# A 90-degree rotation of an 8192x8192 matrix: macro tiles of 512 whole rows in place of 1024 half rows

## The chip, the core and the metric

The kernel runs on one core of a Trainium2 chip. The metric is the device time of one execution in microseconds (us), lower being better. The work of the core is spread over engines that run beside each other, each with its own queue of instructions in a fixed order: TensorE (PE; loading its weights is listed apart as PEld), VectorE (DVE), ScalarE (ACT), GpSimd (POOL) and SyncE (SP). Transfers between the main memory and the on-chip memory (SBUF) are issued by SP and ACT and carried out by 16 DMA engines, which both share. Everything waits for each other through semaphores.

## The reference

The input is a matrix of 8192x8192 float32 numbers (268.44 MB), and the output is the matrix turned by 90 degrees against the clock.

```python
def setup_inputs():
    return {"x": np.random.randn(8192, 8192).astype(np.float32), "k": 1}

def reference(x, k):
    return np.rot90(x, k)
```

So `out[M-1-c, r] = x[r, c]`: a column of the input becomes a row of the output, and the last column becomes the first row. Nothing is computed on the numbers; each is read once and written once, 536.87 MB in all.

## The kernel before

**Macro tiles.** The matrix is cut into macro tiles of `R` = 1024 rows by `W` = 4096 columns, 16 MB each, in `macro_tiles`. There are 16 of them; the last is cut into two of 512 rows (`LAST = [4, 4]`, in units of 128 rows). A macro tile is loaded whole before most of its output can be stored, because a stored run holds one value from each of its rows.

**Load.** `load` brings in 128 rows at a time. Each load (L102, issued by SP) moves 128 rows of 16 KB, 2 MB, into a landing tile `a`, one row to a partition. VectorE then copies the tile in 8 chunks of 512 columns into tiles `ar` (L108), reversing the order of the columns inside each block of 128. In what follows this copy is called a flip.

**Store.** `store` goes over the 32 blocks of 128 columns of a macro tile, `G` = 4 blocks to an output tile. For each block TensorE transposes the eight 128x128 squares (L148) into a PSUM tile `pt`; a PSUM tile holds `PW` = 2 blocks, 2048 numbers to a partition, half of PSUM. ScalarE copies it into the output tile `ot` (L169), and after the second copy it issues the store of 2 MB (L177). Each partition holds 16 KB of the output tile, which goes to four output rows: four runs of 1024 numbers, 4 KB. `whole_reads` (L23) rewrites the reading side of each store from four pieces to one contiguous piece of 16 KB to a partition; the writing side keeps its four runs. With `rows` = 512, in the two last macro tiles, an output tile has 8 blocks, and each partition writes eight runs of 2 KB.

**Buffers.** `a_pool` has 2 landing tiles of 16 KB to a partition, `r_pool` 63 flipped chunks of 2 KB, `o_pool` 3 output tiles of 16 KB, `psum_pool` 2 tiles of 8 KB. A macro tile has 64 chunks, one more than `r_pool` holds. A buffer is taken again as soon as its last reader is done, in the order in which buffers come free. So a load waits until the flips of the load two before it are done; a flip waits for its load and for the transposes that read the buffer it takes; a transpose waits for its flips and for a free PSUM tile; the copies of an output tile wait for the transposes and for the landing of the store that used the buffer before, which is the store three before.

**The two ends.** In the first macro tile some loads land in tiles of `o_pool` (L97), the transposes of the first output tile run row block by row block as these land (L158), and two of the first stores are split in halves (L139). In the two last macro tiles every other output tile is taken from `a_pool` (L131), the flips of the last rows are put ahead of the second output tile (L190 to L200), and the last store is split in halves.

Of the kernel before, what the change touches and what calls it, by code (L numbers as in the profile page):

```python
# [2 lines left out]

# [5 lines left out]

P = 128  # L10

R = 1024
RT = R // P
LAST = [4, 4]
W = 4096
CH = 512
F = 4096  # L20
FP = 2048


def whole_reads(nc):

    for fn in nc.m.functions:
        for block in fn.blocks:
            for n, ins in enumerate(block.instructions):
                if not isinstance(ins, mybir.InstDMACopy):
                    continue
                src = ins.ins[0]
                ap = [list(d) for d in src.ap]
                if len(ap) == 3 and ap[2][0] == 1 and ap[1][0] == ap[2][1]:
                    ap = [ap[0], [1, 1], [1, ap[1][1] * ap[2][1]]]
                    block.instructions[n] = copy.replace(  # L40
                        ins,
                        ins=[copy.replace(src, ap=ap)],
                        ant_dge_precooked=False,
                    )


def macro_tiles(N, M):

    tiles = [(r0, RT, c0) for r0 in range(0, N, R) for c0 in range(0, M, W)]
    r0, _, c0 = tiles.pop()  # L50
    for n in LAST:
        tiles.append((r0, n, c0))
        r0 += n * P
    return tiles


@with_exitstack
def kernel(
    ctx: ExitStack,
    tc: tile.TileContext,  # L60
    x: bass.AP,
    k: bass.AP,
    out: bass.AP,
):
    nc = tc.nc
    assert k == 1, f"only k=1 supported, got {k}"
    nc.at_finalize(whole_reads)

    N, M = x.shape
    dt = x.dtype  # L70

    consts = ctx.enter_context(tc.tile_pool(name="consts", bufs=1))
    ident = consts.tile([P, P], dt)
    make_identity(nc, ident)

    a_pool = ctx.enter_context(tc.tile_pool(name="a_pool", bufs=2))
    r_pool = ctx.enter_context(tc.tile_pool(name="r_pool", bufs=63))
    o_pool = ctx.enter_context(tc.tile_pool(name="o_pool", bufs=3))
    psum_pool = ctx.enter_context(
        tc.tile_pool(name="psum", bufs=2, space=bass.MemoryType.PSUM)  # L80
    )

    loads = 0

    def load(r0, rt, c0):

        nonlocal loads
        chunks = {}
        for t in range(rt):


            if loads < RT and loads % 5 >= 2:  # L97
                a = o_pool.tile([P, W], dt, tag="o")
            else:
                a = a_pool.tile([P, W], dt, tag="a")  # L100
            loads += 1
            nc.sync.dma_start(  # L102
                out=a[:], in_=x[r0 + t * P : r0 + (t + 1) * P, c0 : c0 + W]
            )
            yield chunks
            for j in range(W // CH):
                ar = r_pool.tile([P, CH // P, P], dt, tag="ar")
                nc.vector.tensor_copy(  # L108
                    out=ar[:],
                    in_=a[:, j * CH : (j + 1) * CH].rearrange(  # L110
                        "r (b m) -> r b m", m=P
                    )[:, :, ::-1],
                )
                chunks[t, j] = ar
            yield chunks

    def store(r0, rt, c0, chunks, end):

        rows = rt * P
        PW = 1
        while 2 * PW * rows <= FP:
            PW *= 2
        G = PW
        while 2 * G * rows <= F:
            G *= 2
        for i, g0 in enumerate(range(0, W // P, G)):  # L130
            if end and i % 2 == 0:  # L131
                ot = a_pool.tile([P, F], dt, tag="a")
            else:
                ot = o_pool.tile([P, F], dt, tag="o")
            o = ot[:, : G * rows].rearrange("m (g f) -> m g f", g=G)

            lead = r0 == 0 and c0 == 0 and i in (4, 6)  # L139
            S = PW if lead or (end and r0 + rows == N and g0 + G == W // P) else G  # L140


            ps = {}

            def transposes(t, ws):
                for w in ws:
                    g = g0 + w
                    nc.tensor.transpose(  # L148
                        ps[w // PW][:, PW - 1 - w % PW, t * P : (t + 1) * P],
                        chunks[t, g * P // CH][:, g % (CH // P), :],  # L150
                        ident,
                    )

            def psum_tile(h):
                pt = psum_pool.tile([P, FP], mybir.dt.float32, tag="ps")
                ps[h] = pt[:, : PW * rows].rearrange("m (g f) -> m g f", g=PW)

            if i == 0 and (rt == RT or r0 + rows < N):  # L158
                for h in range(G // PW):
                    psum_tile(h)  # L160
                for t in range(rt):
                    transposes(t, range(G))
            for h in range(0, G, PW):
                if h // PW not in ps:
                    psum_tile(h // PW)
                    for w in range(h, h + PW):
                        for t in range(rt):
                            transposes(t, [w])
                nc.scalar.copy(o[:, G - PW - h : G - h, :], ps[h // PW])  # L169

                done = h + PW
                if done % S == 0:
                    top = M - c0 - (g0 + done) * P
                    dst = out[top : top + S * P, r0 : r0 + rows].rearrange(
                        "(g m) f -> m g f", g=S
                    )
                    nc.scalar.dma_start(  # L177
                        out=dst, in_=o[:, G - done : G - done + S, :]
                    )
            yield  # L180

    tiles = macro_tiles(N, M)
    *most, before_last, last = tiles
    for m in most:
        *_, chunks = load(*m)
        for _ in store(*m, chunks, False):
            pass


    *_, chunks = load(*before_last)  # L190
    outputs = store(*before_last, chunks, True)
    rows = load(*last)
    for _ in range(2 * last[1] - 1):
        next(rows)
    next(outputs)
    chunks = next(rows)
    for _ in outputs:
        pass
    for _ in store(*last, chunks, True):
        pass  # L200


# [1 line left out]
_INS = ['x', 'k']  # L204
_OUTS = [((8192, 8192), 'float32')]

_NUMBERS = {'k': 1}


# [26 lines left out]
```

## Time and profile before

The time is the median of 2 runs. The profile is of one execution of the same program; its span runs from its first to its last instruction.

| | |
|---|---|
| time, median (lowest to highest) | 1267.76 us (1267.45 to 1268.06) |
| span of the profiled execution | 1266.1 us |
| read and written | 268.44 MB and 268.44 MB, 424 GB/s over the span |
| PE, 4096 transposes | busy 718.2 us, 57% of the span |
| PE weight loads, 4096 | busy 678.6 us, 54% |
| ACT, 256 copies of 128x2048, 1869 ns each | busy 466.7 us, 37% |
| DVE, 1024 flips of 128x512 | busy 355.4 us, 28% |
| DVE waits for loads | 524.0 us in 82 waits |
| loads: 128 of 2 MB | 16.8 us from issue to landing (median) |
| stores: 125 of 2 MB, 6 of 1 MB | 25.5 and 27.3 us from issue to landing (median) |

How to read it: busy time is the time in which an engine works on an instruction, and an engine that is idle is waiting for a semaphore. A DMA is issued in well under a microsecond by SP or ACT; its landing is the moment at which the last of the 16 DMA engines has reported. The profile also records each packet, the piece that one DMA engine moves at a time: here one row of 16 KB of a load, or the 16 KB of one partition of a store (8 KB for a half store), and one small packet of 4 bytes for each DMA and DMA engine that reports the landing. A DMA of 128 rows is 8 packets for each of the 16 engines.

### The profile page before, as it was taken

The page shows a single profiled execution, that of the slowest core. Times are in us where ns is not written, and L with a number is a line of the kernel's source. Part 1 is how long each engine was busy: PE and PEld are TensorE (multiplying, and loading weights), DVE is VectorE, ACT ScalarE, POOL GpSimd, SP SyncE. Part 2 cuts the span into 40 slices and gives each one's busy share as a digit, 9 for nine tenths or more (in the row PEclk, how much of TensorE's full clock was granted, in tenths as well). Part 3 has the DMA queues.
Part 4 walks back from the last instruction along what each step waited for, and adds up shares of the span by engine and source line. Part 5 has one row for each costly group of instructions (what it writes and reads, how often), then busy time and mean ns, then how long its engine had stood idle before and what let it go on. Part 6 is the DMA issues. An engine that isn't in the chain of part 4 may idle for free.

```text
span 1266.1 us, 10392 instructions
## 1 busy us (share of the span) xinstructions
PE 718.2 (57%) x4096; PEld 678.6 (54%) x4096; DVE 355.4 (28%) x1024; ACT 466.7 (37%) x257; POOL 0.7 (0%) x6
## 2 busy tenths in 40 slices
PE   1554565556656665556555665555655656556673
PEld 1543455555555555456554655555655655556562
DVE  4423223222232223222232223322232222322210
ACT  0432433433333333343334333343333433343363
POOL 0000000000000000000000000000000000000000
PEclk9977877777776777867778678677686686776797
DMA  9999999999999999999999999999999999999997
GB/s 399 426 428 430 428 429 427 430 429 429 429 429 429 430 428 427 430 429 430 428 430 428 429 429 428 430 428 428 430 430 428 429 429 428 428 428 428 427 399 328
DMA packets 37345, 537.55 MB, mean 425 GB/s; under 512 B 4144, under 2 KB 4144, under 8 KB 4144
## 3 DMA queue, kind: packets, MB, share of 16 engines
q10 hardware_dynamic: 18864, 268.44, 50.0%
q1 hardware_dynamic: 18432, 268.44, 49.7%
q8 instruction: 32, 0.52, 0.2%
q14 instruction: 17, 0.14, 0.0%
HBM read 268.44 MB, written 268.44 MB: 424 GB/s over the span
## 4 chain that ended last, share of the span: by engine, by line
DMA 82%; ACT 14%; PE 1%; issue 1%; ACTq 1%; DVE 0%; SPq 0%
DMA out_dram<-ot 79%; ACT ot L169 14%; DMA a<-in_x_dram 3%; PE pt L148 1%; ACTq L177 0%; DVE ar L108 0%; ACTq L169 0%; SPq L102 0%
## 5 line engine op out<-in xcount | busy, mean ns | idle before, releaser
L148 PE MATMUL pt<-ident,ar 128*128 128x128 f32 x4096 | 718.2, 356 | 528.0 <-ACT ot L169 487.6
L148 PEld LDWEIGHTS pt<-ident,ar 128*128 128x128 f32 x4096 | 678.6, 191 | 567.4 <-ACT ot L169 521.4
L169 ACT COPY ot<-pt 128x2048 f32<-128x2048 f32 x256 | 465.4, 1869 | 756.7 <-DMA out_dram<-ot 727.0
L108 DVE COPY ar<-a 128x512 f32<-128x512 f32 x1024 | 355.4, 421 | 861.1 <-DMA a<-in_x_dram 524.0
L169 ACT ACT_TABLE_LOAD x1 | 1.3, 1283 | 25.5 <-DVE ar L108 25.5
masks.py:199 POOL TENSOR_SCALAR_AFFINE_SELECT ident<-ident 128x128 f32<-128x128 f32 x1 | 0.3, 292 | 0.1
masks.py:197 POOL MEMSET ident<- 128x128 f32 x1 | 0.2, 204 | 0.3 <-POOLq L217 0.3
L217 POOL MEMSET const-bfloat16-1.0<- 128x1 bf16 x1 | 0.1, 102 | 0.0
L217 POOL MEMSET const-uint8-127<- 128x1 uint8 x1 | 0.1, 102 | 0.0
L217 POOL MEMSET const-float32-0.0<- 128x1 f32 x1 | 0.1, 99 | 0.2 <-issue 0.2
L217 POOL MEMSET const-float32-1.0<- 128x1 f32 x1 | 0.1, 99 | 0.0
## 6 DMA issues: line engine op xcount, KB each, us to landing
a<-in_x_dram SPq DMA_DIRECT2D x128, 2048.0 KB, 16.8
out_dram<-ot ACTq DMA_DIRECT2D x125, 2048.0 KB, 25.5
out_dram<-ot ACTq DMA_DIRECT2D x6, 1024.0 KB, 27.3
```

The costliest lines, as they stand in the source:

```text
L108: nc.vector.tensor_copy(out=ar[:], in_=a[:, j * CH : (j + 1) * CH].rearrange("r (b m) -> r b m", m=P)[:, :, ::-1],)
L148: nc.tensor.transpose(ps[w // PW][:, PW - 1 - w % PW, t * P : (t + 1) * P], chunks[t, g * P // CH][:, g % (CH // P), :], ident,)
L169: nc.scalar.copy(o[:, G - PW - h : G - h, :], ps[h // PW])
L217: nc = _bacc.Bacc("TRN2", target_bir_lowering=False, num_devices=1)
```

## The change

Macro tiles become 512 whole rows: `R` = 512 and `W` = 8192, still 16 MB. `macro_tiles`, `LAST` and the special treatment of both ends go, and the two generators become one plain loop.

- A load moves 128 rows of 32 KB, 4 MB; there are 64 instead of 128. The landing tiles are 32 KB to a partition, still two. A load gives 16 chunks.
- An output tile has `G` = 8 blocks, a PSUM tile `PW` = 4; in bytes both are as before. Each of the 128 stores is 2 MB: 16 KB read from each partition, written as eight runs of 2 KB.
- `r_pool` has 55 chunks instead of 63, `o_pool` two tiles instead of three.
- The counts of flips (1024), transposes (4096) and copies (256) and their shapes stay. In the built program each engine has the same instructions in number; SP has 64 loads, ACT 128 stores, none of them half a store.
- The transposes of an output tile always run block by block, over the four row blocks of a block.

```diff
-R = 1024
+R = 512
 RT = R // P
-LAST = [4, 4]
-W = 4096
+W = 8192
...
-    r_pool = ctx.enter_context(tc.tile_pool(name="r_pool", bufs=63))
-    o_pool = ctx.enter_context(tc.tile_pool(name="o_pool", bufs=3))
+    r_pool = ctx.enter_context(tc.tile_pool(name="r_pool", bufs=55))
+    o_pool = ctx.enter_context(tc.tile_pool(name="o_pool", bufs=2))
...
+    PW = FP // R
+    G = F // R
+    for r0 in range(0, N, R):
         chunks = {}
+        for t in range(RT):
+            a = a_pool.tile([P, W], dt, tag="a")
+            nc.sync.dma_start(out=a[:], in_=x[r0 + t * P : r0 + (t + 1) * P, :])
             for j in range(W // CH):
                 ar = r_pool.tile([P, CH // P, P], dt, tag="ar")
                 nc.vector.tensor_copy(
...
                 chunks[t, j] = ar
+        for g0 in range(0, W // P, G):
+            o = o_pool.tile([P, G, R], dt, tag="o")
             for h in range(0, G, PW):
+                pt = psum_pool.tile([P, PW, R], mybir.dt.float32, tag="ps")
+                for w in range(PW):
+                    g = g0 + h + w
+                    for t in range(RT):
+                        nc.tensor.transpose(
+                            pt[:, PW - 1 - w, t * P : (t + 1) * P],
+                            chunks[t, g * P // CH][:, g % (CH // P), :],
+                            ident,
+                        )
+                nc.scalar.copy(o[:, G - PW - h : G - h, :], pt[:])
+            top = M - (g0 + G) * P
+            nc.scalar.dma_start(
+                out=out[top : top + G * P, r0 : r0 + R].rearrange(
+                    "(g m) f -> m g f", g=G
+                ),
+                in_=o[:],
+            )
```

More of the change, by code (lines that the diff above doesn't have):

```diff
@@ L44, in whole_reads @@
                     )
[L47 to L54, printed above, removed]
 @with_exitstack
@@ L81 @@
     )
-    loads = 0
-    def load(r0, rt, c0):
-        nonlocal loads
+    PW = FP // R
+    G = F // R
+    for r0 in range(0, N, R):
         chunks = {}
[L94 to L105, printed above, removed]
+        for t in range(RT):
+            a = a_pool.tile([P, W], dt, tag="a")
+            nc.sync.dma_start(out=a[:], in_=x[r0 + t * P : r0 + (t + 1) * P, :])
             for j in range(W // CH):
@@ L114, in load @@
                 chunks[t, j] = ar
[L115 to L162, printed above, removed]
-            for h in range(0, G, PW):
[L164 to L200, printed above, removed]
+        for g0 in range(0, W // P, G):
+            o = o_pool.tile([P, G, R], dt, tag="o")
+            for h in range(0, G, PW):
+                pt = psum_pool.tile([P, PW, R], mybir.dt.float32, tag="ps")
[15 more added lines that the diff above has]
+            )
```

## The prediction

> **What bounds the kernel now.** I read the page first: its slices and its table of DMA queues.
>
> ```profile
> DMA  9999999999999999999999999999999999999997
> q10 hardware_dynamic: 18864, 268.44, 50.0%
> q1 hardware_dynamic: 18432, 268.44, 49.7%
> ```
>
> The 16 DMA engines are busy from the first slice to the last. The stores (q10, issued by ACT) and the loads (q1, issued by SP) take 99.7% of the span between them, packet after packet. No compute engine comes near: the fullest, PE, is at 57%. So the time is the sum of the packets' times on a DMA engine, and it falls only if packets get shorter and rises if they get longer or if the DMA engines are left without work.
>
> The table of waits says the same from the other side.
>
> ```profile
> ACT ot L169 <- DMA out_dram<-ot: 727.0, 118, 11.0
> PE pt L148 <- ACT ot L169: 487.6, 128, 9.2
> ```
>
> ACT waits for a store to land and frees its output tile, PE waits for ACT. Each of these waits is harmless as long as other packets are queued meanwhile. That is what three output tiles buy, and the change takes one away. So the third view is the timeline of one output tile in the steady part.
>
> ```profile
> 1137.41 3.64 ACT L169 COPY ot<-pt 128x2048 f32<-128x2048 f32 x2 [6.20 <-DMA out_dram<-ot]
> 1139.33 5.14 PEld L148 LDWEIGHTS pt<-ident,ar 128*128 128x128 f32 x32 [3.45 <-ACT ot L169]
> 1141.08 0.55 ACTq L177 DMA_DIRECT2D out_dram<-ot  x1
> 1144.83 2.77 DVE L108 COPY ar<-a 128x512 f32<-128x512 f32 x8 [7.07 <-PE pt L148]
> 1147.24 3.63 ACT L169 COPY ot<-pt 128x2048 f32<-128x2048 f32 x2 [6.19 <-DMA out_dram<-ot]
> ```
>
> An output tile takes 9.83 us (1137.41 to 1147.24), the time of one load and one store on a DMA engine. From the start of the copies to the issue of the store are 3.67 us. Last, the DMA view of four windows: the steady part, the end, where only stores with 2 KB runs are left, and a stretch with half stores beside loads.
>
> ```profile
> DMA packets 2938, 42.89 MB, mean 429 GB/s; under 512 B 320, under 2 KB 320, under 8 KB 320
> q10 hardware_dynamic: 1469, 21.45, 50.5%
> q1 hardware_dynamic: 1465, 21.38, 50.0%
> ```
>
> ```profile
> DMA packets 519, 7.54 MB, mean 419 GB/s; under 512 B 59, under 2 KB 59, under 8 KB 59
> q10 hardware_dynamic: 518, 7.52, 100.4%
> ```
>
> ```profile
> q1 hardware_dynamic: 238, 3.39, 61.2%
> q10 hardware_dynamic: 285, 2.18, 39.7%
> ```
>
> The first, 400 to 500 us: 21.45 MB of stores are 1309 packets of 16 KB, and 50.5% of 16 engines in 100 us is 808 us, so a store packet with 4 KB runs takes 617 ns. The loads give 613 ns. The second, 1226 to 1244 us: 459 packets in 100.4% of 288 us, 629 ns for a store packet with 2 KB runs (most are 626, where most with 4 KB runs are 615). The third, 88 to 101 us: 8 KB store packets beside 16 KB load packets, and the loads got 61% of the time. The engines alternate packet by packet, not byte by byte: the longer packet gets the larger share.
>
> **Loads: 32 KB packets.** The most frequent packet records are 309 ns for 8 KB and 611 ns for 16 KB, so 302 ns for each further 8 KB and 7 ns for the packet itself. A 32 KB packet is then 1215 ns instead of 1222 for two. Each DMA engine has 512 of them: 512 x 7 ns = -3.6 us, and 64 landing packets fewer at 9 ns, -0.6 us. In sum -4.2. No packet of 32 KB is in the trace; the ends are 0 (two times 611) and, by the slower 616 ns that load packets average from 1100 to 1200 us, +5.
>
> **Stores: 2 KB runs everywhere.** Of the 1024 store packets of a DMA engine, the 64 of the last two macro tiles have 2 KB runs already. 960 x (629 - 617) ns = +11.5 us. The row for 2 KB is from a stretch without loads, so the cost beside loads is not shown: ends 0 and, by the worst of the final full stores (634 ns on average), +16. I take 11.5, the row of the same shape. The Trainium skill, "DMA: Bandwidth & Descriptors", section Specifications, asks only 512 B for line rate, so by it 2 KB runs would cost nothing and the traffic would come out at -4.2; the measured 629 against 617 disagrees, and the measurement decides.
>
> So traffic alone moves 1266.1 to 1266.1 - 4.2 + 11.5 = 1273.4 us.
>
> **Two output tiles: does the queue run dry?** This is the part that could cost most. In the built program a load can be issued once the flips of the load two before are done, and the last of these needs the 13th transpose of a PSUM tile that starts when ACT has made the first copy of an output tile, that is, when a store has landed. So the landing of every second store starts both the next load and the refill of that output tile. I count from this landing on one DMA engine. The refill: 0.08 us to the copies, 3.64 us of copies, 0.02 to the issue, then the delay to the first packet. Of that I have two rows: the first 2 KB store, issued at 1217.25 with no load queued, reported from the first DMA engine 6.58 us later, and 8 x 0.626 = 5.01 of these are its packets: 1.57 us. The run's first store, issued at 47.90 into a stream of loads, sent its first packet at 51.14: 3.24 us. So the refill takes 5.3 to 7.0 us; I take 5.3, since the queue of the stores is in use when it is issued. In this time the other output tile is in the queue: 8 packets alone, 8 x 0.629 = 5.0 us. That is 0.3 us too few, unless packets of a load lie among them. The load: its issue comes at 0.08 + 1.92 (start of copy to start of PE) + some 2 (13 transposes; 16 took 1.97 us at 54.60) + 0.4 (a flip) = 4.4 us, its first packet 3.0 (steady loads) to 3.8 us (the load issued at 52.24, beside a store) later, near 7.9 us. It then alternates with the refilled store at 1.22 + 0.63 us a pair. If that store started at 5.3, it has four packets done before the load joins, and lands with about three load packets, 3.6 us, left to cover the next refill. But that later start lets the load catch up, and the round after has no cover but its own 5.0 us. So rounds with 0.3 us and rounds with none alternate; and 16 engines must now report before one of two tiles is free, where the landings of one store are spread over 16 us (the store at 1141.08 was reported from 9.4 to 25.7 us after issue) and the 32 packets that fetch instructions hold one engine up by about 1 us each. I take 0.2 us a round, ends 0 and 1.9 (7.0 - 5.0 in every round). The Trainium skill, same page and section, gives a first byte after about 0.6 us for DMAs of these two queues; the trace has 1.0 at its fastest (the first load, 0.74 to 1.74), and by the rule the refill would be 4.3 us, under 5.0, with no gap at all.
>
> A round is one load and two stores. Loads 0 to 4 go before the first store (5 x 9.7 us, to about 50 us, as 5 to 10 loads did before), so 59 rounds: 59 x 0.2 = +11.8 us.
>
> **The ends.** Before, the first store is issued at 47.90. Now load 3 lands near 1.7 + 4 x 9.7 = 40.6, then flip, two PSUM tiles and two copies give about 46.7, and load 4 keeps the DMA engines busy till 50: nothing lost, so the removed special cases at the start cost nothing; without that load they would cost the 6 us between. At the end some ten stores are left without loads, before with tiles of `a_pool` to help, now with two: 0.3 us for each pair, +1.5. ACT stays off the path, two copies and an issue being 4.2 us against 5.0 of packets.
>
> **Landing tiles, chunks, engines.** The flips of a load are paced by four PSUM tiles, 19.7 us, and a load of 4 MB lands some 22 us after the store that released it; its first chunk is needed after the next two stores have landed. So DVE and PE are not late, and 55 chunks cost nothing; if a load came over 5 us later than this, PE would wait for it and the gap would become a load's.
>
> Sum: 1273.4 + 11.8 + 1.5 = 1286.7 us of span. The median of the runs is 1.7 us above the span, so 1288.
>
> **Rivals.** *The output tiles run dry in every round.* With a delay of 3.24 us, or a load that starts early enough to share its packets away, each round has a gap of 0.7 to 1.9 us: 1274.9 + 1.7 + 59 x 0.7 to 1.9 = 1318 to 1389. For it: the wait for a landing is ACT's largest. Against it: loads need 3 us and more to start, which leaves cover. It decides from (1293.1 - 1276.6) / 59 = 0.28 us a round, where 2% is passed. *The rows pay.* 2 KB runs cost nothing beside loads and no gap opens: 1266.1 - 4.2 + 1.7 = 1264. For it: in the steady part stores share every moment with loads. Against: the 4 KB runs cost their 4 ns more than loads there too. *The 32 KB rows are cut in two by the hardware.* Then loads and stores alternate in equal packets, a store beside a load lasts 10 us, more than any refill: no gap, 1266.1 + 11.5 + 1.7 = 1279.
>
> A gain of 2% is hardly to be had: at 302 ns for 8 KB with nothing for packets, 536.87 MB over 16 engines take 1237 us, 1242 with the ends.
>
> **Chances.** The forecast with a gap of 0 to 0.5 us a round, 1274 to 1306, has 0.55; dry in every round 0.27; the rows pay 0.08; cut in two 0.09; something unseen and faster 0.01. Of the forecast's 0.55 about 0.15 lies above 2%, which is about what a measurement of this kernel can tell from no change. So slower 0.42, same 0.57, faster 0.01. The range, 1268 to 1325, leaves out most of the rows that pay and the worse half of the dry rounds.
>
> **What would show it.** Load packets of 32 KB near 1215 ns and store packets near 629; alternation of pairs in which loads take two thirds; a round of 19.8 us, with a store landing after about 15 us beside a load and 5 alone; a DMA row with tenths of 9 and a few of 8. Slices of 8 throughout would speak for dry rounds; store packets of 617 would show the second term wrong; 64 loads with 16384 packets of 16 KB, the third rival; waits of PE for DVE, the part on chunks.

## The result and the profile after

The changed kernel takes 1379.9 us (median of 2 runs, 1378.4 to 1381.4) against 1267.8 before: 1.0885 times as long, 95% interval 1.0854 to 1.0917. The forecast was 1288, in a range from 1268 to 1325. The profiled execution has a span of 1376.6 us, 110.5 more than before.

The page of the changed kernel, slices and table of DMA queues (packets, MB, share of 16 engines' span):

```profile
DMA  9999999999999999999999999999999999999988
GB/s 410 408 382 393 374 396 407 388 382 381 401 400 386 388 370 401 405 394 383 390 392 409 381 386 385 393 408 384 380 387 396 407 382 386 383 396 418 392 373 344
q10 hardware_dynamic: 18432, 268.44, 48.5%
q1 hardware_dynamic: 9216, 268.44, 47.2%
```

The row of tenths still shows 9 nearly everywhere, and that is a trap: a 9 begins at 90%. The queues tell more. Before, they filled 99.9% of the span, now 95.8% with the instruction fetches (0.1%). Added up from the packet records, the average DMA engine has 56 us without a packet, where it was 2, and 1320 us of packets, where it was 1264: the packets themselves take longer. So about half of the loss, 54 us, is idle time, and the other half, 56 us, is packet time. The load packets average 1268 ns, though the middle one takes 1214; the store packets average 651 ns, though the middle one takes 624.

From the table of waits (us in total, times, longest):

```profile
ACT o L101 <- DMA out_dram<-o: 784.5, 95, 15.1
DVE ar L82 <- PE pt L96: 694.8, 211, 16.2
PE pt L96 <- ACT o L101: 676.5, 122, 15.0
```

ACT's wait for landings grew from 727.0 us in 118 waits to 784.5 us in 95: fewer waits, longer ones, up to 15.1 us where 11.0 was the longest. The landings no longer come evenly. The timeline shows in what order they come (start, duration, engine; in brackets the idle time before and what ended it):

```profile
590.09 0.33 SPq L79 DMA_DIRECT2D a<-in_x_dram  x1
...
601.59 0.55 ACTq L103 DMA_DIRECT2D out_dram<-o  x1
...
603.37 41.49 SPq L79 DMA_DIRECT2D a<-in_x_dram  x3
...
614.30 3.63 ACT L101 COPY o<-pt 128x2048 f32<-128x2048 f32 x2 [12.75 <-DMA out_dram<-o]
...
627.31 3.64 ACT L101 COPY o<-pt 128x2048 f32<-128x2048 f32 x2 [9.38 <-DMA out_dram<-o]
...
630.98 0.55 ACTq L103 DMA_DIRECT2D out_dram<-o  x1
...
632.94 1.87 ACT L101 COPY o<-pt 128x2048 f32<-128x2048 f32 x1 [2.00 <-PE pt L96]
...
637.12 0.55 ACTq L103 DMA_DIRECT2D out_dram<-o  x1
...
640.48 3.64 ACT L101 COPY o<-pt 128x2048 f32<-128x2048 f32 x2 [3.39 <-DMA out_dram<-o]
```

Before, copies started every 9.83 us. Here they start at 614.3, 627.3, 632.9 and 640.5, and the pattern repeats every 42.9 us on average with two loads and four stores, where packets of the middle lengths would need 39.4 (16 x 1.214 + 32 x 0.624). The two loads come close together: one was issued at 590.09, the next at 603.37 (its row merges three issues, of which the others are at 632.76 and 644.53), and both had landed by 626.6. The next one sends its first packet near 638. Two windows of the DMA view, 604 to 609 and 625 to 637 us, show both halves of the pattern:

```profile
q1 hardware_dynamic: 48, 1.57, 72.8%
q10 hardware_dynamic: 35, 0.57, 26.7%
```

```profile
q10 hardware_dynamic: 302, 4.42, 95.6%
q1 hardware_dynamic: 6, 0.00, 0.0%
```

While loads are queued they take two thirds of the engines and more: 73% in this short window, 66.4% from 600 to 624 us, where 207 load packets and 208 store packets were sent, one for one. Stores crawl meanwhile: the store issued at 601.59 took 25.6 us to land. Then for 12 us no load moves at all (the six packets of the second window only report a landing). In the packet records there are 29 such stretches of more than 2.5 us, 382 us in all; before there were two, of 3.5 and 4.0 us, both in the first 140 us. In the 29 two output tiles must keep 16 DMA engines busy alone. Near 631 us they don't: by 631.2 all engines but one had sent their packets of one store, and the next, issued at 630.98, sent its first packet at 632.2.

### The profile page after: what moved, and what is told of

It reads as the page before. It is cut to its first block, busy times and chain, and to the rows that moved or that the text cites. A ratio compares the mean times of both kernels' runs of the same rounds, so it can differ in the third digit from the quotient of the medians.

```text
span 1376.6 us, 10332 instructions
## 1 busy us (share of the span) xinstructions
PE 648.7 (47%) x4096; PEld 615.2 (45%) x4096; DVE 366.1 (27%) x1024; ACT 468.8 (34%) x257; POOL 0.7 (0%) x6
## 3 DMA queue, kind: packets, MB, share of 16 engines
q1 hardware_dynamic: 9216, 268.44, 47.2%
## 4 chain that ended last, share of the span: by engine, by line
DMA 81%; ACT 10%; issue 8%; PE 1%; DVE 0%; ACTq 0%; SPq 0%
DMA out_dram<-o 78%; ACT o L101 10%; DMA a<-in_x_dram 3%; PE pt L96 1%; DVE ar L82 0%; ACTq L101 0%; SPq L79 0%
## 5 line engine op out<-in xcount | busy, mean ns | idle before, releaser
L96 PE MATMUL pt<-ident,ar 128*128 128x128 f32 x4096 | 648.7, 334 | 717.2 <-ACT o L101 676.5
L96 PEld LDWEIGHTS pt<-ident,ar 128*128 128x128 f32 x4096 | 615.2, 177 | 750.5 <-ACT o L101 707.7
L101 ACT COPY o<-pt 128x2048 f32<-128x2048 f32 x256 | 467.5, 1870 | 898.9 <-DMA out_dram<-o 784.5
L82 DVE COPY ar<-a 128x512 f32<-128x512 f32 x1024 | 366.1, 422 | 962.0 <-PE pt L96 694.8
L101 ACT ACT_TABLE_LOAD x1 | 1.3, 1283 | 0.7 <-PEq L125 0.7
```

The costliest lines, as they stand in the source:

```text
L82: nc.vector.tensor_copy(out=ar[:], in_=a[:, j * CH : (j + 1) * CH].rearrange("r (b m) -> r b m", m=P)[:, :, ::-1],)
L96: nc.tensor.transpose(pt[:, PW - 1 - w, t * P : (t + 1) * P], chunks[t, g * P // CH][:, g % (CH // P), :], ident,)
L101: nc.scalar.copy(o[:, G - PW - h : G - h, :], pt[:])
```

## The experiments

Three theories stood at first: that two output tiles are too few (1), that the 32 KB landing tiles and packets make loads come in bursts (2), that 2 KB runs slow the packets beside loads (3). Ratios are to the kernel before in the same comparison, with 95% intervals.

**e1: the kernel before with two output tiles.**

```diff
-    o_pool = ctx.enter_context(tc.tile_pool(name="o_pool", bufs=3))
+    o_pool = ctx.enter_context(tc.tile_pool(name="o_pool", bufs=2))
```

> The kernel before with two output tiles in place of three, nothing else changed. Theory 1 (two output tiles are too few: from the landing of a store to the first packet of the next store from that tile are some 5 us, as from 627.2 to 632.2 us of the changed kernel, and the one other store does not always cover that): the loss of the change comes back here, 1 to 1.75 us for every two stores, 64 times, so 1330 to 1380 us. Theory 2 (the 32 KB landing tiles and packets are to blame: loads come in bursts and leave stretches with stores alone, in which two output tiles are too few; with 2 MB loads always among the stores two would do): 1268 to 1285 us. Theory 3 (2 KB runs): 1268 us, since the runs here are 4 KB.

Measured: 1272.8 us, ratio 1.0047 (1.0032 to 1.0062). The page's queues:

```profile
q10 hardware_dynamic: 18864, 268.44, 49.9%
q1 hardware_dynamic: 18432, 268.44, 49.7%
```

As full as before: two output tiles alone cost 5 us, and theory 1 falls as the sole cause.

**e2: the changed kernel with loads of half rows into four landing tiles of 16 KB.**

```diff
-            a = a_pool.tile([P, W], dt, tag="a")
-            nc.sync.dma_start(out=a[:], in_=x[r0 + t * P : r0 + (t + 1) * P, :])
+            for c0 in range(0, W, AW):     # AW = 4096, a_pool bufs=4
+                a = a_pool.tile([P, AW], dt, tag="a")
+                nc.sync.dma_start(
+                    out=a[:], in_=x[r0 + t * P : r0 + (t + 1) * P, c0 : c0 + AW]
+                )
...
```

The flips of each half follow its load, inside the new loop.

> The changed kernel with its loads cut in two: four landing tiles of 16 KB in the memory of the two of 32 KB, 128 loads of 2 MB in half rows. Output tiles, chunks, macro tiles and 2 KB runs stay. Theory 1: two output tiles stay, so the loss stays, 1340 to 1385 us. Theory 2: loads are released in smaller steps and share the DMA engines packet by packet, so the loss goes, 1275 to 1295 us. Theory 3: as the changed kernel, 1370 to 1390 us.

Measured: 1280.7 us, ratio 1.0106 (1.0089 to 1.0123). The same two output tiles, macro tiles and runs, and 99 of the 112 us are gone. Theory 2 holds in its outline; it has to be told what about the 32 KB does it.

**e3: as e2, with the buffers of the kernel before** (two landing tiles of 16 KB, `r_pool` 63, `o_pool` 3).

> The changed kernel's macro tiles and 2 KB runs with the buffers of the kernel before: two landing tiles of 16 KB, 63 chunks, three output tiles. Theories 1 and 2 alike: only the 2 KB runs and the plain ends are left of the change, 960 store packets on each DMA engine at up to 12 ns, +11.5 us and some us at the end, 1275 to 1290 us. Theory 3 (2 KB runs beside loads are what stretches packets, to 651 ns for stores and 1268 ns for loads on average): 1310 us or more, with store packets of 640 ns or more.

Measured: 1283.5 us, ratio 1.0127 (1.0112 to 1.0142). Theory 3 falls: its 16384 store packets average 626 ns, where it expected 640 or more.

**e4: the changed kernel with four output tiles of 8 KB.**

```diff
-F = 4096
+F = 2048
-    o_pool = ctx.enter_context(tc.tile_pool(name="o_pool", bufs=2))
+    o_pool = ctx.enter_context(tc.tile_pool(name="o_pool", bufs=4))
```

> The changed kernel with four output tiles of 8 KB in the memory of its two of 16 KB: 256 stores of 1 MB, 8 KB packets, still 2 KB runs; landing tiles of 32 KB, loads of 4 MB and 55 chunks stay. Theory 1: while one tile is refilled three others hold packets, 7.5 us of them alone, more than the 5 us of a refill less one of its two copies, so the idle time goes: 1285 to 1310 us, what is left being packets that stretch where a load joins. Theory 2: the loads still come in bursts and take even more of the engines (32 KB against 8 KB a turn), 1340 us or more. Theory 3: 1360 us or more.

Measured: 1299.0 us, ratio 1.0255 (1.0233 to 1.0277). In the same memory, four tiles mend most of it as well, and theory 1's range for this run (1285 to 1310) holds it. The packet records show 37 stretches without loads here, 364 us, so the bursts are still there, but four small tiles let the stores live through them where two large ones don't. Theory 2 expected 1340 us or more and was too simple: it takes bursts and two output tiles together. Load packets still average 1247 ns.

**e5: each load as two DMAs of half rows, into the same landing tile of 32 KB.** This leaves the length of the packets as the cause (2a) or the coarse reloading of the landing tile (2b).

```diff
-            nc.sync.dma_start(out=a[:], in_=x[r0 + t * P : r0 + (t + 1) * P, :])
+            for c0 in range(0, W, W // 2):
+                nc.sync.dma_start(
+                    out=a[:, c0 : c0 + W // 2],
+                    in_=x[r0 + t * P : r0 + (t + 1) * P, c0 : c0 + W // 2],
+                )
```

> The changed kernel with each load issued as two DMAs of half rows into the same 32 KB landing tile: packets are 16 KB, but a landing tile is still reloaded only when its 16 flips are done. Theory 2a (the 32 KB packet: it takes two turns' worth of a DMA engine for each store packet, so loads race ahead and then leave the stores alone): the loss goes, 1275 to 1295 us. Theory 2b (the size of the landing tile: both loads of 4 MB are in, and nothing is left to load until 16 flips are done, which wait for chunks that the transposes free): the loss stays, 1350 to 1390 us, with stretches without loads as before.

Measured: 1281.4 us, ratio 1.0112 (1.0095 to 1.0129). The DMA view from 600 to 643 us, first of this kernel, then of the changed one:

```profile
DMA packets 1255, 18.28 MB, mean 425 GB/s; under 512 B 139, under 2 KB 139, under 8 KB 139
q10 hardware_dynamic: 624, 9.08, 50.4%
q1 hardware_dynamic: 629, 9.18, 50.0%
```

```profile
DMA packets 867, 16.83 MB, mean 391 GB/s; under 512 B 96, under 2 KB 96, under 8 KB 96
q10 hardware_dynamic: 578, 8.42, 49.0%
q1 hardware_dynamic: 288, 8.39, 47.5%
```

The same tiles, chunks and output tiles; only the DMA is cut in two, and the engines are full again. 2b falls.

**e6: the changed kernel with 50 chunks in place of 55** (`r_pool` bufs=50).

> The changed kernel with 50 flipped chunks in place of 55: in the built program the flip that frees a landing tile then waits for a transpose 17 places later, one PSUM tile. Theory 2b: each load is issued later by the time of one PSUM tile, half an output tile, so the stretches without loads grow, and the time with them: 1390 us or more. Theory 2a: the chunks are no limit, 1375 to 1385 us.

Measured: 1372.3 us, ratio 1.0834 (1.0818 to 1.0851). Later flips do no harm; if anything it is 8 us better, which neither theory said.

**e7: one DMA to a load, but its access pattern cut into two pieces of 16 KB to a row.** e5 also let the first half of a load land by itself, so that its flips could start sooner (2c). Here the packets are short and the landing is whole. The last step of the build, where `whole_reads` rewrites the stores, rewrites the loads too:

```diff
+                if ap == [[W, P], [1, W]]:
+                    ap = [[W, P], [W // NP, NP], [1, W // NP]]     # NP = 2
+                    block.instructions[n] = copy.replace(
+                        ins,
+                        ins=[copy.replace(src, ap=ap)],
+                        outs=[copy.replace(ins.outs[0], ap=ap)],
+                        ant_dge_precooked=False,
+                    )
+                    continue
```

> The changed kernel with each load still one DMA of 4 MB with one landing, but described as two pieces of 16 KB to a row, so that its packets are 16 KB. In e5 the first half of a load also landed by itself, and its flips could start earlier; here they can't. Theory 2a (the length of the packet in a turn): as e5, 1275 to 1290 us, packets of 16 KB in the load queue, no stretches without loads. Theory 2c (the earlier landing of the first half did it in e5): 1350 to 1385 us.

Measured: 1298.2 us, ratio 1.0244 (1.0229 to 1.0259), between the two theories but near 2a: 82 of the 99 us that e5 won back come with the shorter packets, under one landing. The other 17 us are not idle time (5 us an engine here, 3 in e5) but packets that take longer, 1291 us an engine against 1276 in e5. Whether that is due to the later landing is not shown; e5 also issues twice as many DMAs.

**e8: the same with four pieces of 8 KB** (`NP = 4`), so that now the store packets are the longer ones.

> The same with four pieces of 8 KB to a row: now a store packet of 16 KB takes two thirds of each pair of turns. Theory 2a: loads are never ahead, so stores are never left alone; the packets cost 7 ns more for each 16 KB of loads, 1024 x 7 ns = 7 us on each DMA engine: 1282 to 1297 us. If any inequality of the packets is harmful, whichever side it favours: 1330 us or more. Theory 2c: 1350 us or more.

Measured: 1377.8 us, ratio 1.0865 (1.0837 to 1.0893). As bad as the change itself, from the other side. From the table of waits:

```profile
DVE ar L92 <- DMA a<-in_x_dram: 784.4, 61, 21.1
ACT o L111 <- DMA out_dram<-o: 447.9, 90, 9.5
ACT o L111 <- PE pt L106: 442.8, 38, 45.0
PE pt L106 <- DVE ar L92: 358.8, 33, 18.5
```

ACT still waits for landings, but no longer for more than 9.5 us. The long waits now run the other way: flips wait for loads, up to 21.1 us, PE for flips, ACT for PE, and the stores stop: in the packet records 15 stretches of more than 2.5 us without stores, 249 us. As in the changed kernel, the idle engines are only a part of the loss: against e5 they are 33 us of it, and 66 us are packet time, of which the shorter packets themselves explain some 10 (at the middle lengths, 311 ns for 8 KB and 612 for 16 KB). So 2a as it was written, that only a lead of the loads does harm, is wrong; its alternative in the same expectation, that any inequality does, is what came.

**e9: e4 with loads in pieces of 8 KB**, equal to its store packets of 8 KB.

> The kernel of e4 (four output tiles of 8 KB, store packets of 8 KB; 1299 us, packets of loads stretched to 1247 ns where 1214 is the rule) with loads in pieces of 8 KB: both sides' packets equal again. Theory 2a: loads and stores flow evenly, the stretched packets go; on each DMA engine 2048 load packets at 309 ns and 2048 store packets at 315 ns, 1278 us, and the ends: 1283 to 1293 us, under e4. Theory 2c: 1299 us as e4, or more by the 11 us of the extra packets.

Measured: 1282.0 us, ratio 1.0114 (1.0097 to 1.0131), 17 us under e4 and just below 2a's range of 1283 to 1293, though it has four times as many load packets (33792 with the landing packets, against 9216).

**e10: the kernel before with loads in two pieces of 8 KB.** The rewriting is that of e7, with rows of 16 KB; everything else is the kernel before.

> The kernel before with its loads described in two pieces of 8 KB to a row, so that a store packet of 16 KB now takes two thirds of each pair of turns; all buffers stay (two landing tiles of 16 KB, three output tiles). e8 showed that packets of unequal length cost as much when they favour the stores. If that holds for any kernel with two or three buffers on each side, loads fall behind, PE waits for flips, and stores stop meanwhile: 1300 to 1370 us. If it takes the change's two output tiles, only the packets' own cost remains, 1024 x 7 ns = 7 us on each DMA engine: 1270 to 1280 us.

Measured: 1331.2 us, ratio 1.0501 (1.0483 to 1.0519). From the table of waits:

```profile
DVE ar L118 <- DMA a<-in_x_dram: 903.4, 125, 13.1
ACT ot L179 <- PE pt L158: 526.6, 61, 31.8
PE pt L158 <- DVE ar L118: 387.1, 63, 13.1
ACT ot L179 <- DMA out_dram<-ot: 247.1, 63, 4.8
```

The same chain as in e8. The kernel before has three output tiles and loses 64 us to nothing but shorter load packets, of which their own cost explains 7. By the packet records 24 of the 64 us are idle engines and 40 are packet time. The stores stop in 15 stretches, 309 us in all, and there the load packets, alone on the engines, average 351 ns, against 311 elsewhere. Its speed hung on 16 KB against 16 KB.

**e11: whole-row macro tiles with three landing tiles of 16 KB and three output tiles**, equal packets.

> The whole-row macro tiles with three landing tiles of 16 KB and three output tiles, 55 chunks, 128 loads of half rows: equal packets and one buffer more on the store side than e2 (1281 us). If what is left over the kernel before is the 2 KB runs and the plain ends alone, 1276 to 1284 us, the same as e2; if two output tiles still cost something there, 1270 to 1276 us.

Measured: 1279.6 us, ratio 1.0091 (1.0076 to 1.0106). As e2: what is left over the kernel before is the runs and the ends, not the buffers. No version with whole rows came under the kernel before.

## Why the prediction was wrong

The point lay 92 us low and the result outside the range; slower by over 2% had 0.42 and came. The sum, term by term:

- **Traffic, +7.3 us: about right.** A load packet of 32 KB takes 1214 ns, the middle one, where 1215 were worked out. The store packets with 2 KB runs have a middle of 624 ns; in e2 they average 624 against 617 before, 7 ns where 12 were taken. Measured without bursts, in e2, e5 and e11, the new macro tiles and runs stand at 1279.6 to 1281.4 us. By the 7 ns e2 would be at 1266.1 + 7.5 + 1.7 = 1275; of the 5 us above that, 4 are idle engines in its last 60 us (12 us there, 8 before), so the plain end costs more than the 1.5 that were taken. The Trainium skill, "DMA: Bandwidth & Descriptors", section Specifications, asks only 512 B for line rate; by it the 2 KB runs would cost nothing, and here they cost 7 ns a packet.
- **"I take 0.2 us a round": this is the step that failed.** What is left of the measured time after traffic and ends, 1379.9 - 1276.6 = 103 us, is 1.75 us for each of 59 rounds. Some 53 of it are idle engines, 0.9 us a round where 0.2 were taken; the ends given, 0 and 1.9, held that, and the value was chosen near the wrong one. The rest, some 49 us, are packets that took longer than their middle length, for which the sum had no term at all. The refill itself was sized about right: from the landing at 627.2 to the next store's first packet at 632.2 are 5.0 us, where 5.3 were taken. What failed is the cover. The choice rested on a picture in which each round has one load beside one refilled store, with load packets left over as cover. In the trace the rounds go in pairs: two loads run one behind the other and land by 626.6, and then 12 us pass without any load, in which the cover is nothing but the other output tile.
- **The row that decided it was in the prediction.** The stretch with half stores beside loads was read rightly: engines alternate packet by packet, the longer packet gets the larger share (61% there, 66.4% in the changed kernel, whose middle lengths, 1214 and 611 to 624 ns, give 66%). It was used to count cover within a round, and not for what it does over several rounds: a side that gets two thirds runs ahead until its buffers are full and then leaves the other alone. e5 and e7 show it by cutting the packets, e8 and e10 by turning the inequality round. The Trainium skill, same page, section Queues, rings and completion order, has an engine go round the queues and change only when a packet is done. The records agree, with 207 load packets and 208 store packets from 600 to 624 us; the runs add what it comes to when the packets differ: 1379.9 and 1377.8 us against 1281.4.
- **The third rival gave the right price for the wrong case.** The 32 KB rows are not cut: the page lists 9216 records for the loads, of which 8192 are packets of 32 KB. But what this rival described, equal packets in turn without a gap at 1279 us, is e5, and e5 took 1281.4.
- **The rival of dry output tiles, 1318 to 1389, holds the result, but its mechanism is half of it.** Idle engines are 54 us of the loss. The other 56 us are packet time, of which 7 were foreseen as traffic; the rest are stretched packets, which no case had. In the steady part of the changed kernel the packet records show them where a load joins stores that run alone: from 593 to 595 us store packets average 1.13 us in place of 0.62, then load packets 1.44 us in place of 1.21 until 599. While that lasts no engine is idle, so gaps alone could not have been the whole account. In e5 and e2 loads and stores are queued all the time, and the longer packets are nearly gone with the bursts. Why packets stretch is not shown: in e10 nearly all of the stretched ones are loads in stretches without any store, so a second queue that joins is not the whole answer, and no run was made on it by itself.
- **Chunks, engines and the start: as said.** e6 with fewer chunks is no slower, PE's matmuls wait for flips in 4 places only, 40.4 us in all, and in the first 60 us an engine is without a packet for 2 us in both kernels, so nothing was lost at the start by idle engines.

## What to carry to other kernels

Where two streams of transfers share the DMA engines and depend on each other through a few buffers, look first at the bytes of one packet on each side: the engines take turns by packet, so the packets' lengths set the ratio of the streams. If the work needs 1:1, make the packets 1:1, or give each side the buffers to live through the other's burst: four output tiles in place of two brought 1379.9 us to 1299.0, equal packets 1281.4. And a dose of the same cause with the other sign (e8, e10) told more than removing it: without it "loads race ahead" would have stood as the explanation, when here either side's lead costs about the same (1379.9 and 1377.8 us).

## What the hardware showed that was not expected

- Cutting a DMA's access pattern into pieces changes the length of its packets, with the same bytes and one landing: 1379.9 us with 32 KB, 1298.2 with 16 KB, 1377.8 with 8 KB.
- Packets stretch, most of all in the kernels whose packets are unequal: in the changed kernel load packets average 1268 ns where the middle one is 1214, and store packets 651 where it is 624; in e10 load packets of 8 KB average 351 ns in the stretches without stores, where the middle one is 309. In e7, with equal packets, store packets still average 637. The cause is open.
- Equal bytes at both queues do not mean full engines: in the changed kernel each side has its half of the traffic, and the engines are 4% idle.
